# Chunked SSD steps taken in group pairs, with the first projection's matmuls in one run per pair

## The chip, the cores and the metric

One core of a Trainium2 chip runs the whole kernel as one program. The metric is the device time of one execution in microseconds (us); the median of several runs counts. The engines are TensorE (PE in the profile, PEld for its weight loads), VectorE (DVE), ScalarE (ACT), GpSimd (POOL) and SyncE (SP, which issues the loads).

## The reference

One layer of a decoder trunk with two branches, on x of 1024 positions by 1024 channels, all in float32. One branch is a chunked causal gMLP (spatial gating), the other a Mamba-2 SSD mixer with 8 groups of 4 heads (head size 64, state size 128, chunks of 128 positions). Both are projected, gated and merged:

```python
proj = h @ w_in
gm_u, gm_v, gm_z, ssm_z, xbc, dt_raw, g_a, g_b = jnp.split(proj, SPLITS, axis=-1)
y_a = spatial_gating(gelu(gm_u), gelu(gm_v), ...) * silu(gm_z)
xbc = silu(causal_depthwise_conv(xbc, conv_w, conv_b))
xs, bm, cm = jnp.split(xbc, ...)
y_b = ssd_scan(xh, dt, a, bm, cm) + xh * d_skip[:, None]
y_b = rms_norm per group (y_b * silu(ssm_z))
merged = sigmoid(g_a) * (y_a @ w_proj_a) + sigmoid(g_b) * (y_b @ w_proj_b)
return x + gate * (merged @ w_out)        # then a final rms_norm
```

and the scan, per chunk and group:

```python
cb = einsum('bclgn,bcsgn->bcgls', cc, bc)
y_diag = einsum('bcgls,bcgrls,bcsgrp->bclgrp', cb, decay, xd)
chunk_states = einsum('bcsgn,bcgrs,bcsgrp->bcgrpn', bc, decay_to_end, xd)
state = state * chunk_decay + chunk_states                  # from chunk to chunk
y_off = einsum('bclgn,bcgrpn,bcgrl->bclgrp', cc, prev_states, exp(a_cs))
y = y_diag + y_off
```

## The kernel before

**Stages.** First the input projection runs, feature-major, as pairs of column blocks multiplied in a scheme of seven products (p1 to p7). Its products are finished on ScalarE and VectorE and stored in DRAM: `s_d` holds a slab per group and chunk pair (C, B, two blocks of x, two of z), `acs_d` the running sums of the decay, `th_d` the gates, `ya_d` the gMLP's result. Then come the SSD steps, with `y_a @ w_proj_a` (the *first projection*) between them. Then the second projection in seven products (its matmuls are on L1433), the merge, and the output projection. Large products in float32 are taken as three products of a high and a low part.

**The SSD steps.** A step is one group and one pair of chunks (256 positions); there are 32. `order` (L1095) takes two groups side by side: (0,0), (1,0), (0,1), (1,1), and so on, so a group's successive steps are two apart, since the state runs from chunk to chunk. A step has these parts:

- `fetch` (L936): SP loads `dcy` (512 KB, the sums broadcast to all partitions) and `sl`, the slab (768 KB). There are five sets of buffers, so a fetch waits until the step five before is through with its set.
- `decay` (L952): ScalarE makes `ea` (L957), POOL masks dcy (affine select, L960), ScalarE takes the exponentials of dcy in eight pieces (L965).
- `prep` (L967): TensorE multiplies C and B into `pc` and transposes B and x into `pc` and `px`; VectorE scales x into `xd` and `xe` (L981) and multiplies dcy by pc (L985); ScalarE copies B into `bn` (L987).
- `front` (L990): TensorE multiplies `yi` from xd and dcy, and `sp`, the chunks' state sums, from bn and xe; POOL decays the state (L1013) and VectorE adds sp (L1015), for each of the two chunks.
- `back` (L1019): TensorE multiplies `yn` from the states; VectorE makes y1 = yi + D x (L1041) and ym (L1045); POOL adds them and multiplies by z (L1046, L1047), giving `yz`. After a group's odd chunk pairs `post` stores yz as `yb_d` (issued by ScalarE, L88), and squares and sums for the norm follow by the list of later work (`pq`, L1074).

**The first projection** (`proj_a`, L1243) is a generator. A block of 128 output rows takes 24 pieces; a piece is two matmuls `pma` of 128x512, one per half of the positions. At a block's start SP loads `tha` (the gate, two tiles from a ring) and weights; at its end VectorE multiplies tha by pma (L1266) and ScalarE issues the store to `mt_d` (L1268). `draw(n)` takes n pieces.

**What sets the order.** The program is written in the order that L1303 to L1323 says, and a scheduler places it on each engine; parts of a step are marked as urgent. Per step n: its front, four or five pieces (ten for the first three), its back, the preparation of step n + 2, the fetch up to step n + 5, the decays up to n + 3. What remains of the first projection is drawn behind the last step. Each engine works through its own list in order. PSUM has eight banks, handed out in turn by `bank`.

**Places.** The [128, 512] tiles of the stage come from one list of free slots (`room`); `ring(n)` takes n of them and `turn` hands them out in turn: four for tha, three for ea, two each for y1 and ym (L1272). A chunk's state tile is 256 wide and takes, in turn, a slot of its own and places in two other pools (L1273).

Of the kernel before, what the change touches and what calls it, by code (L numbers as in the profile page):

```python
# [8 lines left out]
F32 = mybir.dt.float32  # L9
# [3 lines left out]
ALU = mybir.AluOpType  # L13
# [3 lines left out]
P = 128  # L17
# [18 lines left out]
def hybrid_kernel(  # L36
# [7 lines left out]
    V, A, G, PE = nc.vector, nc.scalar, nc.gpsimd, nc.tensor  # L44
# [25 lines left out]
    def cst(shape, name, dt=F32):  # L70
        return const.tile(shape, dt, name=name, tag=name)
# [3 lines left out]
    def mm(acc, l, r, first=True, last=True):  # L75
        pin(PE.matmul(acc, l, r, start=first, stop=last))  # L76
# [7 lines left out]
    def load(dst, src):  # L84
        pin(nc.sync.dma_start(dst, src))
# [28 lines left out]
    dskt = cst([P, 16], "dskt")  # L114
# [16 lines left out]
    hp = hpool.__enter__()  # L131
# [335 lines left out]
    def bank(name):  # L467

        if pairs_done:
            pairs_done.append(name)  # L470
            if len(pairs_done) % 4 == 2:
                return psum.tile([P, 512], F32, name=name, tag="px", bufs=2)
        return psum.tile([P, 512], F32, name=name, tag="bk", bufs=6)
# [449 lines left out]
    def fac(t, g, s):  # L923

        return t.rearrange("p (c h) -> p c h", h=NH)[:, 2 * s : 2 * s + 2, HPG * g : HPG * (g + 1)]

    NSET = 5
    nstep, nst = [0], [0]

    class Group:  # L930
# [5 lines left out]
        def fetch(self, s):  # L936
            g, nm = self.g, f"{self.g}_{s}"
            n = nstep[0] % NSET
            nstep[0] += 1
            pool, b = (p2r, 2) if n < 2 else (p2q, NSET - 2)  # L940
            dcy = pool.tile([P, HPG, 2, P], F32, name=f"dcy{nm}", tag="dcy", bufs=b)
            load(dcy.rearrange("p h i l -> p (h i l)"),
                 acs_d[g, s].rearrange("h t -> (h t)").unsqueeze(0).to_broadcast([P, HPG * 256]))
            sl = pool.tile([P, 6, 256], F32, name=f"sl{nm}", tag="sl", bufs=b)
            load(sl, s_d[g][:, s])
            if n < 2:
                ea = p2r.tile([P, 2, 256], F32, name=f"ea{nm}", tag="ea", bufs=2)
            else:
                ea = turn(ea_r, f"ea{nm}", F32).rearrange("p (j t) -> p j t", j=2)
            self.pre[s] = (sl, dcy, ea)  # L950
# [39 lines left out]
        def front(self, s):  # L990

            g, nm = self.g, f"{self.g}_{s}"
            sl, dcy, bn, xd, xe, ea = self.pre[s]
            v3 = lambda t: t.rearrange("p (h w) -> p h w", h=HPG)
            yi = bank(f"yi{nm}")
            for i in range(2):
                for h in range(HPG):
                    j, hh = h // 2, h % 2
                    mm(yi[hh * HD : (hh + 1) * HD, j * 256 + i * P : j * 256 + (i + 1) * P],
                       xd[:, i * 256 + h * HD : i * 256 + (h + 1) * HD], dcy[:, h, i, :])  # L1000
            sp = bank(f"sp{nm}")
            self.y[s] = yi
            self.sts = [self.st]
            for i in range(2 if s < NCH // 2 - 1 else 1):
                mm(sp[:, i * 256 : (i + 1) * 256], bn[:, i * P : (i + 1) * P], xe[:, i * 256 : (i + 1) * 256])
            for i in range(2 if s < NCH // 2 - 1 else 1):
                pool, tag, b = st_r[nst[0] % 4 if nst[0] % 4 < 3 else 2]
                nst[0] += 1
                s2 = pool.tile([P, 512 if pool is hp else 256], F32, name=f"st{nm}_{i}", tag=tag, bufs=b)[:, 0:256]
                if self.st is None:  # L1010
                    V.tensor_copy(s2, sp[:, 0:256])
                else:
                    G.tensor_mul(v3(s2), v3(self.st),  # L1013
                                 fac(cd, g, s)[:, i].unsqueeze(2).to_broadcast([P, HPG, HD]))
                    V.tensor_add(s2, s2, sp[:, i * 256 : (i + 1) * 256])  # L1015
                self.st = s2
                self.sts.append(s2)

        def back(self, s):  # L1019

            sl = self.pre[s][0]
            yn = bank(f"yn{self.g}_{s}")
            for i in range(2):
                if self.sts[i] is not None:
                    for j in range(2):
                        mm(yn[:, j * 256 + i * P : j * 256 + (i + 1) * P], self.sts[i][:, j * P : (j + 1) * P],
                           sl[:, 0, i * P : (i + 1) * P])
            self.evacuate(s, self.y.pop(s), yn)
            if s % 2:
                self.post(s // 2)  # L1030

        def evacuate(self, s, yi, yn):

            g, nm = self.g, f"{self.g}_{s}"
            sl, ea = self.pre[s][0], self.pre[s][5]
            if s % 2 == 0:
                self.yz[s // 2] = p2r.tile([P, 2, 512], F32, name=f"yz{nm}", tag="w4", bufs=4)
            yz = self.yz[s // 2][:, :, (s % 2) * 256 : (s % 2 + 1) * 256]
            y1 = turn(y1_r, f"y1{nm}", F32).rearrange("p (j t) -> p j t", j=2)
            for j in range(2):  # L1040
                V.scalar_tensor_tensor(y1[:, j], sl[:, 2 + j], dskt[:, 2 * g + j : 2 * g + j + 1],  # L1041
                                       yi[:, j * 256 : (j + 1) * 256], op0=ALU.mult, op1=ALU.add)
            m = turn(ym_r, f"ym{nm}", F32).rearrange("p (j t) -> p j t", j=2)
            t0 = 0 if s else P
            V.tensor_tensor(m[:, :, t0:], yn.rearrange("p (j l) -> p j l", j=2)[:, :, t0:], ea[:, :, t0:], op=ALU.mult)  # L1045
            G.tensor_add(y1[:, :, t0:], y1[:, :, t0:], m[:, :, t0:])  # L1046
            G.tensor_mul(yz, y1, sl[:, 4:6])  # L1047
# [47 lines left out]
    order = [(2 * r + j, s) for r in range(NG // 2) for s in range(4) for j in range(2)]  # L1095
# [8 lines left out]
    def decays(n):  # L1104
        while done_d[0] < min(n, len(order)):
            g, s = order[done_d[0]]
            groups[g].decay(s)
            done_d[0] += 1
# [18 lines left out]
    room = [f"{nm}{v}{k}" for nm in BN for v in "hl" for k in range(4)]  # L1127

    def take(name, tag=None, dt=F32R):
        return hp.tile([P, 512], dt, name=name, tag=tag or room.pop(0))  # L1130

    def ring(n):

        return [room.pop(0) for _ in range(n)], [0]

    def turn(r, name, dt=F32R):
        tags, at = r
        at[0] += 1
        return take(name, tags[(at[0] - 1) % len(tags)], dt)
# [63 lines left out]
    for n, (name, _, _, d1, d2, g) in enumerate(todo):  # L1203
# [21 lines left out]
        if n + 2 == len(todo):  # L1225
            wspool.__exit__(None, None, None)
            p2xpool = tc.tile_pool(name="p2x", bufs=1, side="right", reuse_waits="tile")
            p2x = p2xpool.__enter__()
# [12 lines left out]
    p2q = p2qpool.__enter__()  # L1241
# [27 lines left out]

    for r in (war_r, wah_r, wal_r):  # L1270
        r[0][0].extend(room.pop(0) for _ in range(2))
    tha_r, ea_r, y1_r, ym_r = (ring(c) for c in (4, 3, 2, 2))  # L1272
    st_r = [(hp, room.pop(0), 1), (p2x, "st", 1), (p2q, "st", 2)]  # L1273
    fetch(4)
    wa_load(1)
    fetch(5)
# [13 lines left out]
    def draw(n):  # L1290
        for _ in range(n):
            left[0] -= next(fill, 1) is None

    def item(f, s):
        with tc.high_priority():
            f(s)
        run_tasks()

    def step(n, *fs):
        for f in fs:  # L1300
            item(getattr(groups[order[n][0]], f), order[n][1])

    draw(6)  # L1303
    for n in range(2):
        step(n, "front")
        draw(10)
    for n in range(len(order)):
        if n > 1:
            step(n, "front")
            draw(10 if n == 2 else 4 + n % 2)  # L1310
        step(n, "back")
        if n + 2 < len(order):
            step(n + 2, "prep")
        fetch(n + 6)
        decays(n + 4)
    while tasks:
        draw(2)
        run_tasks()


    room.extend(ea_r[0] + [st_r[0][1]])
    room.extend(tag for k in range(KT - 2) for tag in ya_tags[k])
    draw(left[0] - 5)  # L1323

# [14 lines left out]
    def slot_tile(name, dt=F32):  # L1339
        tag = room.pop(0)  # L1340
        t = hp.tile([P, 512], dt, name=name, tag=tag)
        tags_of[name] = tag
        return t
# [165 lines left out]
    for u, (nm, k) in enumerate(units):  # L1509
# [22 lines left out]
        if nm in ("p7", "p4") and k % 2 == 0:  # L1532
            n = k // 2 + (4 if nm == "p4" else 0)
# [7 lines left out]
        if k == KT - 1:  # L1541
            for j in range(4):
                with tc.high_priority():
                    if nm == "p1":
                        t = slot_tile(f"c11_{j}")
# [4 lines left out]
                    elif nm in ("p5", "p3"):  # L1550
                        t = slot_tile(f"{nm}_{j}")
# [130 lines left out]
```

## Time and profile before

| | us |
|---|---|
| median of 3 runs | 1427.75 (1426.89 to 1429.42) |
| the profiled execution | 1430.48 |
| its span in the trace | 1428.8 |
| TensorE busy | 1398.2 (98%) |
| VectorE busy | 1025.1 (72%) |
| ScalarE busy | 783.3 (55%) |
| POOL busy, nearly all of it in the SSD stage | 200.0 (14%) |
| mean granted clock of TensorE | 0.997 |

The span runs from the first to the last instruction that the profiler recorded; the execution's own time has 1.7 us more around it. A row of the timeline reads: start in us, length of the group, engine, line, operation, output and inputs with the buffers' numbers left out, sizes, count; in brackets the idle time just before it, and what ended it. A row of the waits reads: engine, what waited, on whom; us in total, how many times, the longest.

### The profile page before, as it was taken

The page shows a single profiled execution, that of the slowest core. Times are in us where ns is not written, and L with a number is a line of the kernel's source. Part 1 is how long each engine was busy: PE and PEld are TensorE (multiplying, and loading weights), DVE is VectorE, ACT ScalarE, POOL GpSimd, SP SyncE. Part 2 cuts the span into 40 slices and gives each one's busy share as a digit, 9 for nine tenths or more (in the row PEclk, how much of TensorE's full clock was granted, in tenths as well). Part 3 has the DMA queues.
Part 4 walks back from the last instruction along what each step waited for, and adds up shares of the span by engine and source line. Part 5 has one row for each costly group of instructions (what it writes and reads, how often), then busy time and mean ns, then how long its engine had stood idle before and what let it go on. Part 6 is the DMA issues. An engine that isn't in the chain of part 4 may idle for free.

```text
span 1428.8 us, 20531 instructions
## 1 busy us (share of the span) xinstructions
PE 1398.2 (98%) x7111; PEld 1157.7 (81%) x7111; DVE 1025.1 (72%) x1812; ACT 783.3 (55%) x1436; POOL 200.0 (14%) x188
## 2 busy tenths in 40 slices
PE   8999999999999999999999999999999999999997
PEld 7788888888888888888888788878888877787886
DVE  4686677777677888788888884488677766948443
ACT  5664576666556655545665555767667533334201
POOL 0000000000000000000000100048878810000000
PEclk9999999999999999999999999999999999999999
DMA  8552333333323687587687764799788567987332
GB/s 268 150 169 82 126 106 108 102 113 103 118 87 107 197 237 220 159 251 225 193 240 214 225 190 148 253 310 314 258 264 305 206 226 266 355 262 280 121 118 74
DMA packets 260460, 276.82 MB, mean 194 GB/s; under 512 B 13596, under 2 KB 210628, under 8 KB 260356
## 3 DMA queue, kind: packets, MB, share of 16 engines
q1 hardware_dynamic: 179364, 195.24, 43.9%
q10 hardware_dynamic: 80992, 80.26, 16.6%
q8 instruction: 56, 0.92, 0.3%
q14 instruction: 48, 0.39, 0.1%
HBM read 191.27 MB, written 84.18 MB: 193 GB/s over the span
## 4 chain that ended last, share of the span: by engine, by line
PE 78%; DMA 9%; DVE 5%; issue 3%; ACT 2%; POOL 2%; SPq 1%; ACTq 0%; POOLq 0%; DVEq 0%
PE xuz L560 6%; PE po L76 6%; PE xcb L560 6%; PE xx L560 5%; PE xz L560 5%; PE x L1433 4%; PE xg L560 4%; PE pma L76 3%; PE yp L1433 3%; PE xv L560 3%; PE yuz L560 3%; PE ycb L560 3%; PE yx L560 3%; PE yz L560 2%; DMA yn<-yb_d 2%
## 5 line engine op out<-in xcount | busy, mean ns | idle before, releaser
L766 POOL TENSOR_TENSOR wog<-wog,gb 128x1024 f32<-128x1024 f32 x8 | 20.3, 2536 | 722.8 <-DVE wbr L800 529.3
L965 ACT ACTIVATE dcy<-dcy,nacs 128x128 f32<-128x128 f32 x256 | 78.4, 390 | 13.4 <-POOL dcy L960 13.3
L960 POOL TENSOR_SCALAR_AFFINE_SELECT dcy<-dcy 128x1024 f32<-128x1024 f32 x32 | 35.0, 1095 | 107.9 <-ACT ea L957 107.7
L957 ACT ACTIVATE ea<-dcy 64x512 f32<-64x512 f32 x64 | 40.1, 627 | 11.4 <-DMA dcy<-acs_d 11.0
L1645 ACT ACTIVATE xr<-r 128x1024 f32<-128x1024 f32 x7 | 7.4, 1061 | 67.2 <-issue 39.7
L878 ACT ACTIVATE ac<-ac 128x1024 f32<-128x1024 f32 x32 | 34.0, 1062 | 17.9 <-DVE ac L876 17.8
L76 PE MATMUL pma<-yh,wah 128*128 128x512 f32 x128 | 43.1, 418 | 0.0
L76 PE MATMUL pma<-yh,wal 128*128 128x512 f32 x128 | 42.6, 414 | 0.0
L1045 DVE TENSOR_TENSOR ym<-yn,ea 128x512 f32<-128x512 f32 (+1 forms) x32 | 19.9, 623 | 30.6 <-PE yn L76 30.6
L1047 POOL TENSOR_TENSOR yz<-y,sl 128x512 f32<-128x512 f32 x32 | 41.5, 1298 | 0.9
L985 DVE TENSOR_TENSOR dcy<-dcy,pc 128x1024 f32<-128x1024 f32 x32 | 39.0, 1217 | 3.3 <-PE pc L79 1.9
L76 PE MATMUL pma<-yl,wah 128*128 128x512 f32 x128 | 40.1, 394 | 0.0
L1046 POOL TENSOR_TENSOR y<-y,ym 128x512 f32<-128x512 f32 (+1 forms) x32 | 36.6, 1143 | 16.7 <-DVE ym L1045 16.6
L76 PEld LDWEIGHTS yn<-sl,st 128*128 128x128 f32 x224 | 30.4, 190 | 9.5 <-POOL yz L1067 3.7
L1644 DVE TENSOR_TENSOR r<-po,xr 128x1024 f32<-128x1024 f32 x7 | 8.6, 1225 | 41.1 <-PE po L76 41.1
L876 DVE SCALAR_TENSOR_TENSOR ac<-c2cb,cwt,ac 128x1023 f32<-128x1023 f32 (+2 forms) x24 | 32.0, 1335 | 7.9 <-ACT ac L874 6.4
L76 PE MATMUL yn<-sl,st 128*128 128x128 f32 x224 | 31.8, 277 | 5.8 <-DVE st L1015 4.6
L1372 DVE SCALAR_TENSOR_TENSOR yn<-yn,par,rb 128x512 f32<-128x512 f32 x32 | 24.0, 749 | 17.2 <-DMA yn<-yb_d 17.1
L876 DVE SCALAR_TENSOR_TENSOR ac<-c2x,cwt,ac 128x1023 f32<-128x1023 f32 (+2 forms) x24 | 30.7, 1280 | 7.6 <-ACT ac L874 6.1
L76 PE MATMUL sp<-xe,bn 128*128 128x256 f32 x112 | 32.6, 408 | 2.8 <-DVE xe L981 1.2
L1635 POOL TENSOR_TENSOR r<-r,fnw 128x256 f32<-128x256 f32 (+1 forms) x3 | 2.8, 918 | 232.4 <-ACT xr L1634 232.4
L76 PE MATMUL yi<-dcy,xd 128*64 128x128 f32 x512 | 35.0, 279 | 0.0
(2810 smaller groups left out, 4406.6 us busy)
## 6 DMA issues: line engine op xcount, KB each, us to landing
sl<-s_d SPq DMA_DIRECT2D x32, 768.0 KB
s_d<-ac ACTq DMA_DIRECT2D x32, 512.0 KB
dcy<-acs_d SPq DMA_DIRECT2D x32, 512.0 KB
aw<-in_ada_w_dram SPq DMA_DIRECT2D x16, 512.0 KB
wbr<-in_w_proj_b_dram SPq DMA_DIRECT2D x64, 128.0 KB
wb_d<-wbb ACTq DMA_DIRECT2D x32, 256.0 KB
wb_d<-wbc ACTq DMA_DIRECT2D x32, 256.0 KB
yb_d<-yz ACTq DMA_DIRECT2D x32, 256.0 KB
```

What stands on the lines that cost most here:

```text
L76: pin(PE.matmul(acc, l, r, start=first, stop=last))
L560: pin(PE.matmul(ps, lw[:, k * P : (k + 1) * P], r[k], start=first and n + k == 0, stop=n == 2 and k == 3, skip_group_check=not first))
L876: V.scalar_tensor_tensor(ac[:, s:], cc[:, : S - s], conv_wt[:, 3 - s, i : i + 1], ac[:, s:], op0=ALU.mult, op1=ALU.add)
L878: A.activation(ac, ac, AF.Silu)
L957: A.activation(ea[hh * HD : (hh + 1) * HD], dcy.rearrange("p (j e) i l -> p e j (i l)", e=2)[hh * HD : (hh + 1) * HD, hh], AF.Exp)
L960: G.affine_select(out=d8, in_=d8, compare_op=ALU.is_ge, fill=-1e30, base=0, pattern=[[0, 2 * HPG], [1, P]], channel_multiplier=-1)
L965: A.activation(dcy[:, h, i, :], dcy[:, h, i, :], AF.Exp, bias=sub[:, i, h : h + 1])
L985: V.tensor_tensor(d3, d3, pc[:, 0:256].unsqueeze(1).to_broadcast([P, HPG, 256]), op=ALU.mult)
L1046: G.tensor_add(y1[:, :, t0:], y1[:, :, t0:], m[:, :, t0:])
L1047: G.tensor_mul(yz, y1, sl[:, 4:6])
L1372: V.scalar_tensor_tensor(t, t, snw[:, n : n + 1], rbs[n // 2, h], op0=ALU.mult, op1=ALU.mult)
L1433: pin(PE.matmul(ps[j], a[:, v, js], r, start=first and n + k == 0, stop=n == 2 and k == KT - 1, skip_group_check=not first))
```

## The change

The unit of the loop becomes a pair of steps: the two groups' steps of the same chunk pair. Per pair the program now has front, front, nine pieces of the first projection in one run (14 for the first pair), back, back, the two preparations of the next pair, the fetches up to step n + 6 (n is the pair's first step), and the decays up to n + 5. Six pieces still lie ahead of the first front. In all 155 pieces are drawn in the loops, where it was 167; the rest goes behind the last step.

Three things go with it. y1 is made at the end of `front` and no longer in `evacuate`. The two states of a step lie in the halves of one [128, 512] tile, out of a ring of four (three slots and one place in another pool). And the ring of tha goes from four slots to two, so that the states' slots come out of the same list.

```diff
             sp = bank(f"sp{nm}")
-            self.y[s] = yi
             self.sts = [self.st]
+            nst[0] += 1
+            both = (p2q.tile([P, 512], F32, name=f"st{nm}", tag="st") if nst[0] % 4 == 0 else
+                    take(f"st{nm}", st_r[nst[0] % 4 - 1], F32))
...
-                pool, tag, b = st_r[nst[0] % 4 if nst[0] % 4 < 3 else 2]
-                nst[0] += 1
-                s2 = pool.tile([P, 512 if pool is hp else 256], F32, name=f"st{nm}_{i}", tag=tag, bufs=b)[:, 0:256]
+                s2 = both[:, i * 256 : (i + 1) * 256]
...
+            self.y[s] = y1 = turn(y1_r, f"y1{nm}", F32).rearrange("p (j t) -> p j t", j=2)
+            for j in range(2):
+                V.scalar_tensor_tensor(y1[:, j], sl[:, 2 + j], dskt[:, 2 * g + j : 2 * g + j + 1],
+                                       yi[:, j * 256 : (j + 1) * 256], op0=ALU.mult, op1=ALU.add)
...
-        def evacuate(self, s, yi, yn):
+        def evacuate(self, s, y1, yn):
...
-            y1 = turn(y1_r, f"y1{nm}", F32).rearrange("p (j t) -> p j t", j=2)
-            for j in range(2):
-                V.scalar_tensor_tensor(y1[:, j], sl[:, 2 + j], dskt[:, 2 * g + j : 2 * g + j + 1],
-                                       yi[:, j * 256 : (j + 1) * 256], op0=ALU.mult, op1=ALU.add)
...
-    tha_r, ea_r, y1_r, ym_r = (ring(c) for c in (4, 3, 2, 2))
-    st_r = [(hp, room.pop(0), 1), (p2x, "st", 1), (p2q, "st", 2)]
+    tha_r, ea_r, y1_r, ym_r = (ring(c) for c in (2, 3, 2, 2))
+    st_r = ring(3)[0]
...
     draw(6)
-    for n in range(2):
-        step(n, "front")
-        draw(10)
-    for n in range(len(order)):
-        if n > 1:
-            step(n, "front")
-            draw(10 if n == 2 else 4 + n % 2)
-        step(n, "back")
+    for n in range(0, len(order), 2):
+        for m in range(2):
+            step(n + m, "front")
+        draw(14 if n == 0 else 9)
+        for m in range(2):
+            step(n + m, "back")
         if n + 2 < len(order):
-            step(n + 2, "prep")
-        fetch(n + 6)
-        decays(n + 4)
+            for m in range(2, 4):
+                step(n + m, "prep")
+        fetch(n + 7)
+        decays(n + 6)
...
-    room.extend(ea_r[0] + [st_r[0][1]])
+    room.extend(ea_r[0] + st_r)
```

In the rows below a name such as yi2_2 is the tile yi of group 2, chunk pair 2; the number behind it is a tile's own. First TensorE, around the preparation of a step of chunk pair 2 of groups 2 and 3. Before: the preparation of (2,2), then the front of the step (3,1), which was prepared a step earlier, then the first projection.

```order
L76 MATMUL pc2_2_9542<-sl2_2_9332 128x128
L79 MATMUL pc2_2_9542<-ident_128,sl2_2_9332 128x128
L79 MATMUL px2_2_9541<-ident_128,sl2_2_9332 128x128 x2
L76 MATMUL yi3_1_9576<-dcy3_1_9240,xd3_1_9476 64x128 x8
L76 MATMUL sp3_1_9585<-xe3_1_9478,bn3_1_9481 128x256 x2
L76 MATMUL pma3_0_9604<-yh00_8360,wah3_0_9272 128x512
```

After, from the end of the second preparation of the pair (2,2), (3,2) on:

```order
L76 MATMUL pc3_2_9580<-sl3_2_9448 128x128
L79 MATMUL pc3_2_9580<-ident_128,sl3_2_9448 128x128
L79 MATMUL px3_2_9579<-ident_128,sl3_2_9448 128x128 x2
L76 MATMUL yi2_2_9632<-dcy2_2_9269,xd2_2_9572 64x128 x8
L76 MATMUL sp2_2_9641<-xe2_2_9574,bn2_2_9577 128x256 x2
L76 MATMUL pq0_1_9652<-ones_133,yz0_2_9071 128x1 x4
L76 MATMUL yi3_2_9662<-dcy3_2_9446,xd3_2_9589 64x128 x8
L76 MATMUL sp3_2_9671<-xe3_2_9591,bn3_2_9594 128x256 x2
L76 MATMUL pq1_1_9682<-ones_133,yz1_2_9081 128x1 x4
L76 MATMUL pma2_0_9368<-yh50_8463,wal2_1_9047 128x512
```

A preparation was followed by another step's front; now both fronts follow directly on the two preparations of their own steps, and the run of pma comes behind them.

VectorE at the same place. Before, two steps follow each other, each with its ym, states, and the preparation's three operations:

```order
L1045 TENSOR_TENSOR ym2_1_9535<-yn2_1_9527,ea2_1_9173 128x512
L1015 TENSOR_TENSOR st2_1_1_9516<-st2_1_1_9516,sp2_1_9510 128x256
L985 TENSOR_TENSOR dcy2_2_9330<-dcy2_2_9330,pc2_2_9542 128x1024
L981 TENSOR_TENSOR xd2_2_9551<-px2_2_9541,dthq_147 128x512
L981 TENSOR_TENSOR xe2_2_9553<-px2_2_9541,dde_148 128x512
L1041 SCALAR_TENSOR_TENSOR y13_1_9623<-sl3_1_9242,dskt_144,yi3_1_9576 128x256 x2
L1015 TENSOR_TENSOR st3_1_0_9588<-st3_1_0_9588,sp3_1_9585 128x256
L1045 TENSOR_TENSOR ym3_1_9626<-yn3_1_9618,ea3_1_9244 128x512
L1015 TENSOR_TENSOR st3_1_1_9591<-st3_1_1_9591,sp3_1_9585 128x256
L985 TENSOR_TENSOR dcy3_2_9410<-dcy3_2_9410,pc3_2_9633 128x1024
```

After, the same place holds both ym, then both preparations, then the states and y1:

```order
L1045 TENSOR_TENSOR ym2_1_9545<-yn2_1_9540,ea2_1_9129 128x512
L1045 TENSOR_TENSOR ym3_1_9556<-yn3_1_9551,ea3_1_9268 128x512
L985 TENSOR_TENSOR dcy2_2_9269<-dcy2_2_9269,pc2_2_9563 128x1024
L981 TENSOR_TENSOR xd2_2_9572<-px2_2_9562,dthq_147 128x512
L981 TENSOR_TENSOR xe2_2_9574<-px2_2_9562,dde_148 128x512
L985 TENSOR_TENSOR dcy3_2_9446<-dcy3_2_9446,pc3_2_9580 128x1024
L981 TENSOR_TENSOR xd3_2_9589<-px3_2_9579,dthq_147 128x512
L981 TENSOR_TENSOR xe3_2_9591<-px3_2_9579,dde_148 128x512
L1015 TENSOR_TENSOR st2_2_9642<-st2_2_9642,sp2_2_9641 128x256
L1075 TENSOR_SCALAR ssq_151<-pq0_1_9652 128x4
L1020 SCALAR_TENSOR_TENSOR y12_2_9649<-sl2_2_9271,dskt_144,yi2_2_9632 128x256 x2
L1020 SCALAR_TENSOR_TENSOR y13_2_9679<-sl3_2_9448,dskt_144,yi3_2_9662 128x256 x2
```

The six operations of two preparations now stand in one run between the pair's ym and its own states; y1 has moved ahead of the ym of its step.

SP's loads around the third block of the first projection, before:

```order
L85 DMA wa4_1_9127<-in_w_proj_a_dram 128x4x128
L85 DMA tha2_0_9129<-th_d_107 128x512
L85 DMA tha2_1_9132<-th_d_107 128x512
L85 DMA dcy2_1_9169<-acs_d_57 128x1024
L85 DMA sl2_1_9171<-s_d2_119 128x1536
L85 DMA dcy3_1_9240<-acs_d_57 128x1024
```

and after:

```order
L85 DMA wa4_1_9364<-in_w_proj_a_dram 128x4x128
L85 DMA tha2_0_9366<-th_d_107 128x512
L85 DMA tha2_1_9369<-th_d_107 128x512
L85 DMA dcy3_2_9446<-acs_d_57 128x1024
L85 DMA sl3_2_9448<-s_d3_120 128x1536
L85 DMA dcy2_3_9451<-acs_d_57 128x1024
```

The kinds of loads stand in the same order; the fetches behind tha2 are now those of a later step, and tha2 takes the slots that the block just before it had.

## Prediction

> **What bounds the kernel now.** I read the engine totals first, then the stage that the change touches, then TensorE's waits in it, then a stretch of its timeline beside VectorE's. The page's head gives the span and each engine's busy time:
>
> ```profile
> span 1428.8 us, 20531 instructions
> PE 1398.2 (98%) x7111; PEld 1157.7 (81%) x7111; DVE 1025.1 (72%) x1812; ACT 783.3 (55%) x1436; POOL 200.0 (14%) x188
> ```
>
> TensorE is busy 98% of the span, so the kernel is TensorE's instruction list plus about 30 us of gaps. The SSD steps lie between 928 and 1150 us. Cut into windows (columns: window, length, busy time of PE, PEld, DVE, ACT, POOL, then the granted clock, the DMA share and GB/s):
>
> ```profile
> 928.00:950.00 22.00, 20.11 (x130) 16.52 (x130) 19.33 (x32) 17.38 (x44) 8.73 (x11) 1.00 1.02 351
> 950.00:1000.00 50.00, 48.19 (x370) 41.89 (x369) 39.54 (x70) 34.07 (x89) 37.09 (x36) 1.00 0.86 295
> 1000.00:1050.00 50.00, 47.04 (x356) 40.73 (x355) 35.69 (x67) 35.10 (x93) 39.16 (x38) 1.00 0.74 249
> 1050.00:1100.00 50.00, 47.31 (x370) 41.63 (x369) 36.54 (x68) 34.24 (x91) 40.41 (x39) 1.00 0.87 296
> 1100.00:1150.00 50.00, 48.27 (x373) 41.97 (x372) 35.78 (x68) 27.41 (x69) 39.32 (x39) 1.00 0.57 197
> ```
>
> TensorE idles 1.89 + 1.81 + 2.96 + 2.69 + 1.73 = 11.1 us of these 222. That is all that a better order of this stage can win, 0.8% of the time. Its waits there:
>
> ```profile
> PE yn L76 <- DVE st L1015: 4.6, 4, 2.2
> PE pc L76 <- issue: 1.9, 1, 1.9
> PE sp L76 <- DVE xe L981: 1.2, 2, 0.6
> PE yn L76 <- POOL yz L1067: 1.2, 1, 1.2
> PE sp L76 <- DVE ssq L1075: 1.0, 1, 1.0
> PE sp L76 <- DVE ym L1045: 0.7, 1, 0.7
> PE pq L76 <- ACT bn L987: 0.6, 1, 0.6
> ```
>
> Eleven waits in 32 steps: most steps have none. The next question is what keeps TensorE fed between a preparation and the front that uses it. Two steps of its timeline:
>
> ```profile
> 956.38 1.05 PE L76 MATMUL yn<-sl,st 128*128 128x128 f32 x8
> 957.26 0.39 PE L76 MATMUL pc<-sl 128*128 128x128 f32 x2
> ...
> 958.46 1.09 PE L76 MATMUL yi<-dcy,xd 128*64 128x128 f32 x16
> 959.48 1.13 PE L76 MATMUL sp<-xe,bn 128*128 128x256 f32 x4
> 960.26 0.81 PE L76 MATMUL pma<-yh,wah 128*128 128x512 f32 x2
> ...
> 968.68 1.05 PE L76 MATMUL yn<-sl,st 128*128 128x128 f32 x8
> 969.57 0.39 PE L76 MATMUL pc<-sl 128*128 128x128 f32 x2
> ```
>
> Two steps take 968.68 - 956.38 = 12.30 us. A preparation lasts 958.46 - 957.26 = 1.20 (its transposes end it), yi 959.48 - 958.46 = 1.02, sp 960.26 - 959.48 = 0.78. The yi behind this preparation is of the step before the prepared one; the prepared step's own yi comes one whole step later. VectorE's rows for the same kind of preparation:
>
> ```profile
> 964.79 1.22 DVE L985 TENSOR_TENSOR dcy<-dcy,pc 128x1024 f32<-128x1024 f32 x1
> 965.92 0.68 DVE L981 TENSOR_TENSOR xd<-px,dthq 128x512 f32<-128x512 f32 x1
> 966.52 0.68 DVE L981 TENSOR_TENSOR xe<-px,dde 128x512 f32<-128x512 f32 x1
> 969.77 0.69 DVE L1045 TENSOR_TENSOR ym<-yn,ea 128x512 f32<-128x512 f32 x1 [1.45 <-PE yn L76]
> 970.71 1.22 DVE L985 TENSOR_TENSOR dcy<-dcy,pc 128x1024 f32<-128x1024 f32 x1 [0.25 <-PE pc L79]
> 974.49 1.28 DVE L1266 SCALAR_TENSOR_TENSOR tha<-tha,pma 128x512 f32<-128x512 f32 x2
> ```
>
> dcy, xd and xe start 1.13 and 0.60 us apart. In the old order that chain (some 3 us) has six for itself and costs TensorE nothing.
>
> **The change part by part.** The matmuls are the same, and so are the instructions of the other engines. What moves is who stands between them.
>
> *yi of the pair's first step.* Let T be the start of the first preparation on TensorE. The second follows at once, so TensorE reaches yi at T + 2 x 1.20 = T + 2.4, or 2.3 without the gap ahead of a yi. VectorE's dcy starts 970.71 - 969.57 = 1.14 behind pc, xd 1.13 later, and lasts 0.68: T + 2.95. From a VectorE end to the matmul that waits for it I add 0.1, as at 948.55 below. So yi starts at T + 3.05 and waits 0.75. This is so in 15 of 16 pairs (the first is prepared earlier): **11.2 us**. Nothing of pma is left to lie there, since all nine pieces stand ahead of the backs.
>
> *yi of the second step.* VectorE's second dcy starts at 1.14 + 1.13 + 0.60 + 0.60 = 3.47, its xd ends at 3.47 + 1.13 + 0.68 = 5.28, and yi can start at 5.38. TensorE is there at 3.05 + 1.02 + 0.78 = 4.85, or at 4.46 in the last chunk pair of a group, where sp is half as long. In the fronts of chunk pairs 0 and 2 the sums of squares stand in between, and a row of them covers it:
>
> ```profile
> 989.89 0.95 PE L76 MATMUL pq<-ones,yz 128*128 128x1 f32 x8
> ```
>
> The other eight wait 4 x 0.5 and 4 x 0.9: **5.6 us**.
>
> *Banks.* A pair now holds seven of the eight PSUM banks or more (px, pc, yi and sp of one step while the other's are prepared, two pma), where a step shared them with its neighbour alone. The nearest rows, the two waits of sp for xe above (0.6 each), are of this kind. Between nothing and 0.6 for each of 15 pairs (0 to 9) I take **2.5**, near the few that the rows show.
>
> *Start of the stage.* The wait of 1.9 us in the list above is this one, with VectorE's row before it:
>
> ```profile
> 947.77 0.68 DVE L981 TENSOR_TENSOR xe<-px,dde 128x512 f32<-128x512 f32 x1
> 948.55 0.46 PE L76 MATMUL pc<-sl 128*128 128x128 f32 x2 [1.89 <-issue]
> ```
>
> The preparation for the second pair waits for the first pair's xe (end 948.45). Before, 6 + 10 + 10 pieces lay ahead of the first back; now it is 6 + 14, so six pieces (12 matmuls of 0.23, 2.8 us) fewer cover it. Half of that is filled by the second front and the second back: 1.9 + 1.4 = **3.3** (bounds 1.9 and 4.7).
>
> *Old waits.* Of the other 9.2 us, those of yn for st came of a draw too short for the chain sp, st. Two fronts and nine pieces now lie there, so I keep a quarter, **2.3** (bounds 0 and 9.2).
>
> *SP's queue.* The ring of tha goes from four slots to two. Its next load now waits until the last block's product (DVE L1266 above) has been stored, and every dcy and sl fetch issued later stands behind it. ScalarE's issue of that store, the landing of a store and of a dcy in the chain of waits, and the three operations on a dcy that has landed:
>
> ```profile
> 975.69 0.33 ACTq L1268 DMA_DIRECT2D mt_d<-tha  x1
> 992.98 6.82 DMA yb_d<-yz
> 1007.85 7.38 DMA dcy<-acs_d
> 964.78 1.25 ACT L957 ACTIVATE ea<-dcy 64x512 f32<-64x512 f32 x2
> 969.80 1.09 POOL L960 TENSOR_SCALAR_AFFINE_SELECT dcy<-dcy 128x1024 f32<-128x1024 f32 x1 [1.03 <-ACT ea L957]
> 962.42 2.45 ACT L965 ACTIVATE dcy<-dcy,nacs 128x128 f32<-128x128 f32 x8 [1.77 <-POOL dcy L960]
> ```
>
> From a block's last matmul: product 1.4, issue 1, landing 6.8, so 9.2 until SP is free; then 1 for the two loads, dcy 7.4, ea 1.25, select 1.1, exps 2.45: 22.4 us until that dcy may be multiplied. It belongs to the second step of the next pair, whose turn comes at 12.3 + 3.5 + the pair's own waits of 0.8 = 16.6 behind this pair's T. A block ends 3.5 to 5.8 us ahead of T (pieces left in the draw x 0.46, plus two yn of 1.05), so it is from 0 to 2.3 us late, at five places (the loads of blocks two to six). Half of 2.3 is 1.2 each: **6** (bounds 0, if those stores land in half the time, and 20, if the selects on POOL and the exps on ScalarE that stand behind it in order hold up the states as well).
>
> *At nothing.* The states that share a tile: the same copies, multiplications and additions, and yn still waits for the half that it reads; the cover is the nine pieces (4.2 us), and without it a yn would pay up to the 2.2 of the list. y1 made in the front: the same two VectorE instructions, behind the second xe; VectorE is busy 79% of a window at most from 950 on, and what waits for y1 is POOL's sum behind the backs, nine pieces later.
>
> *The tail.* The loops draw 155 pieces instead of 167; 12 (5.6 us) go behind the last step. The stage behind it waits like this:
>
> ```profile
> 1166.35 0.50 PE L1433 MATMUL x<-p1bh,p1a 128*128 128x512 f32 x1 [1.43 <-DVE tha L1266]
> 1216.91 0.76 PE L1433 MATMUL yp<-p5bh,p5a 128*128 128x512 f32 x1 [2.31 <-issue]
> 1200.00:1250.00 50.00, 47.69 (x199) 37.93 (x198) 46.95 (x75) 16.48 (x28) 0.00 (x0) 0.97 0.99 368
> ```
>
> The first waits for the last product, which stays last, and in 1200 to 1250 VectorE (94%) and the DMA (0.99) are as full as TensorE. More matmuls ahead give VectorE a little lead: **-0.4** (bounds 0 and -3.7, both waits).
>
> *Sum.* 11.2 + 5.6 + 2.5 + 3.3 + 2.3 + 6 = 30.9 us of gaps where 11.1 were, less 0.4: +19.4. The profiled execution took 1430.48 (span 1428.8 and 1.7 around it), 2.7 above the median of 1427.75; gaps carry over from one execution to another, so I add to the median: **1447**.
>
> **The rivals.**
> 1. *Faster.* All of the old 11.1 goes, the tail's 3.7 too, and only the first yi's 11.2 come: 1427.75 - 14.8 + 11.2 = 1424. For it: two fronts and nine pieces cover a state chain better than one and four or five. Against it: eight second fronts whose xd is late by VectorE's own rows. It decides at 14.8 / 15 = 1.0 us of new waits a pair, and VectorE's chain alone gives 0.75. Chance 0.09.
> 2. *The loop through SP, POOL and ScalarE.* A late dcy holds the selects and exps behind it, those hold states and bn, and the next fetches come later again: the 20 for the 6, so 1461. For it: POOL is busy 74 to 81% in these windows and has little to catch up with. Against it: each fetch has a pair's lead. Chance 0.20.
> 3. *The waits are covered*, because VectorE reaches the preparations earlier than its rows say or the scheduler's order leaves other matmuls there: new and old gaps equal, 1428. Against it: the order on TensorE is pc, px, yi without a matmul between. Chance 0.08.
> 4. *The clock.* In the window 1200 to 1250 a wait of 2.31 goes with a granted clock of 0.97, so 0.03 x 50 = 1.5 us; the stage's own windows keep 1.00 with a wait of 2.2 in them. If each of 15 pairs set off such a dip: 22 on top, 1469. Chance 0.03.
>
> The Trainium skill, page "TensorE: Matmul & The Clock Gate", section "HAM oscillation — how this bites in real kernels", wants no idle gap of TensorE above about 3.4 us, because the clock falls behind one; by that rule gaps of 0.75 leave the clock alone, and the rows of 950 to 1150 agree (1.00 with gaps to 2.2). Its section "A second HAM failure mode: psum-queue depth-cycling" speaks against this change: short idles between groups of matmuls, set off by cycling through PSUM banks, made the clock swing there; that is rival 4, and no run here shows it in this stage.
>
> **How the numbers follow.** The forecast has the remaining 0.60; with its terms between their bounds it lies at 1432 to 1459. The range adds rival 2 and leaves out 1, 3 and 4 (0.20): 1431 to 1463. A measurement of this kernel can tell about 0.2% (2.9 us) from no change. Faster by more: rival 1 and a little of 3, 0.10. Within: the rest of 3 and a little of the forecast, 0.09. Slower: 0.81.
>
> **What would show it.** Right: about 15 waits of yi for VectorE's xd (or the bank's xe) near 0.75, eight more at the second yi; yn's waits for st nearly gone; TensorE idle some 31 us in the stage; SP waiting for a store ahead of the tha loads; 12 more pieces behind the last step. Wrong: yi starting right behind px, TensorE idle under 15 us in the stage, or waits of yn and pc larger than those of yi, which would put the cost in fetches and states instead of the missing cover.

## The result, and the profile after

| | before | after |
|---|---|---|
| median, us (4 runs each) | 1428.59 | 1474.57 |
| ratio, 95% interval | | 1.0306 (1.029 to 1.0322) |
| profiled execution, its span, us | 1430.48, 1428.8 | 1474.75, 1473.0 |
| TensorE busy, us | 1398.2 | 1413.6 |
| mean granted clock | 0.997 | 0.986 |

The change costs 46 us, not the 19 that were forecast, and lies above the range. All times and ratios in this document leave out one slow execution (2014.72 us at a granted clock of 0.654, of the run with the squares placed later). The page's head of after:

```profile
span 1473.0 us, 20574 instructions
PE 1413.6 (96%) x7111; PEld 1166.2 (79%) x7111; DVE 1028.1 (70%) x1812; ACT 785.4 (53%) x1436; POOL 197.8 (13%) x188
```

The span grew by 44.2 us. TensorE idles 1473.0 - 1413.6 = 59.4 us of it, where it was 30.6: 28.8 more. The other 15.4 is *busy* time, for the same 7111 matmuls. So a third of the loss is no wait at all: the same instructions took longer. The windows of after (columns as in the prediction's table of windows) say where and why:

```profile
928.00:950.00 22.00, 18.60 (x141) 15.16 (x139) 20.50 (x34) 17.52 (x45) 11.08 (x12) 1.00 0.91 322
950.00:1000.00 50.00, 42.56 (x305) 36.10 (x302) 33.34 (x59) 30.50 (x81) 30.63 (x31) 0.93 0.63 225
1000.00:1050.00 50.00, 43.60 (x312) 37.05 (x312) 31.15 (x56) 26.61 (x68) 32.88 (x33) 0.97 0.70 248
1050.00:1100.00 50.00, 43.75 (x318) 37.79 (x318) 30.66 (x58) 31.71 (x84) 33.94 (x34) 0.93 0.76 265
1100.00:1150.00 50.00, 41.35 (x308) 35.15 (x306) 32.41 (x58) 29.65 (x76) 30.42 (x31) 0.97 0.61 214
1150.00:1200.00 50.00, 46.48 (x273) 39.24 (x272) 22.31 (x42) 12.37 (x30) 25.45 (x24) 0.90 0.39 131
```

The granted clock, 1.00 in every window of this stage before, is still 1.00 in the first and 0.90 to 0.97 in the others. Over the whole span 0.014 of 1473.0 is 20.6 us, and 0.003 of 1428.8 was 4.3: 16.3 us more, close to the extra busy time of 15.4.

The windows of before and after do not hold the same work, since the steps now end later: the last yi runs at 1174 and not at 1146. So here is the whole stage, from 928 to the first product of the second projection (at 1163.42 before, at 1201.34 after), and what follows it, beside the forecast's sum:

| us | before | after | more | forecast |
|---|---|---|---|---|
| the stage, TensorE idle | 11.1 | 37.0 | 25.9 | 19.8 |
| the stage, TensorE busy (1657 matmuls at a granted clock of 1.00, then 1647 at 0.94) | 224.3 | 236.3 | 12.0 | 0 |
| from there to the end of the span | 265.4 | 271.7 | 6.3 | -0.4 |

The waits of TensorE from 928 to 1200:

```profile
PE px L79 <- DVE ym L1045: 7.7, 3, 2.7
PE yi L76 <- DVE xd L981: 7.4, 5, 3.7
PE sp L76 <- ACT bn L987: 6.6, 6, 3.1
PE yi L76 <- issue: 5.4, 5, 2.0
PE yi L76 <- DVE xe L981: 2.7, 2, 1.4
PE yi L76 <- POOL st L1013: 2.0, 2, 1.4
PE yi L76 <- POOL y L1046: 1.9, 3, 0.7
PE yi L76 <- POOL yz L1047: 1.4, 1, 1.4
PE pc L76 <- DVE st L1015: 0.3, 1, 0.3
```

Two things stand in this list. yi waits 18 times, 20.8 us in all, where it never waited before. And px, which should be ready to go, waits three times, over 2.3 us each, for VectorE's ym. The releasers beside yi differ (DVE, POOL, issue), but the place is one: behind the pair's own preparations. (At 1007.45, for one, yi is put down to POOL's y, but VectorE's xd had ended 0.10 before it started.)

The wait of px is worth following back, because it begins on another queue. These rows are of after's timeline, one engine behind the other (the stores that ScalarE issues, SP, ScalarE, POOL, VectorE, TensorE):

```profile
1003.54 0.81 ACTq L1268 DMA_DIRECT2D mt_d<-tha  x2
...
996.51 3.27 SPq L85 DMA_DIRECT2D wa<-in_w_proj_a_dram  x2
1008.15 0.95 SPq L85 DMA_DIRECT2D tha<-th_d  x2
1009.21 0.37 SPq L85 DMA_DIRECT2D dcy<-acs_d  x1
...
1015.71 1.27 ACT L957 ACTIVATE ea<-dcy 64x512 f32<-64x512 f32 x2 [6.23 <-DMA dcy<-acs_d]
1020.54 0.60 ACT L1169 CAST wah<-wa 128x512 fp32r<-128x512 f32 x1
...
1017.05 1.09 POOL L960 TENSOR_SCALAR_AFFINE_SELECT dcy<-dcy 128x1024 f32<-128x1024 f32 x1 [4.97 <-ACT ea L957]
...
1018.76 0.42 DVE L1015 TENSOR_TENSOR st<-st,sp 128x256 f32<-128x256 f32 x1 [5.93 <-POOL st L1013]
1021.17 0.69 DVE L1170 TENSOR_TENSOR wal<-wa,wah 128x512 fp32r<-128x512 f32 x1 [1.99 <-ACT wah L1169]
1021.78 1.28 DVE L1045 TENSOR_TENSOR ym<-yn,ea 128x512 f32<-128x512 f32 x2
...
1022.52 0.44 PE L79 MATMUL px<-ident,sl 128*128 128x128 f32 x2 [2.68 <-DVE ym L1045]
1024.84 1.98 PE L76 MATMUL yi<-dcy,xd 128*64 128x128 f32 x16 [1.34 <-DVE xd L981]
```

SP is through with the weights at 999.8 and stands still until 1008.15: the load of tha waits for the store issued at 1003.54. The dcy behind it is issued at 1009.21 and reaches ScalarE at 1015.7, where ea has waited 6.23. ScalarE works in order, so the cast of the weights behind ea (wah) is late; POOL's select waits 4.97 and the states stand behind it; VectorE's wal waits for the cast, and both ym stand behind wal. The px of the second preparation needs a bank that ym still reads. TensorE waits 2.68, then 1.34 for xd; and the yi that then runs takes 1.98, where the same 16 matmuls took 1.09 before.

The end of the stage shows the same queue once more:

```profile
1168.12 24.40 SPq L85 DMA_DIRECT2D tha<-th_d  x4
1192.62 0.38 SPq L85 DMA_DIRECT2D rb<-rs_d  x1
...
1209.55 0.79 PE L1432 MATMUL x<-p1bh,p1a 128*128 128x512 f32 x1 [5.05 <-DVE tha L1266]
```

The last block's tha holds the first loads of the second projection (rb, yn, p1r) until 1192.62; TensorE gets there at some 1200 and waits 1.54 and 5.05 in its first products, where it waited 1.43 in all. The 5.05 end with the first projection's last product, which VectorE reaches only at 1208.22, behind its work on these late loads.

### The profile page after: what moved, and what is told of

It reads as the page before. It is cut to its first block, busy times and chain, and to the rows that moved or that the text cites. A ratio compares the mean times of both kernels' runs of the same rounds, so it can differ in the third digit from the quotient of the medians.

```text
span 1473.0 us, 20574 instructions
## 1 busy us (share of the span) xinstructions
PE 1413.6 (96%) x7111; PEld 1166.2 (79%) x7111; DVE 1028.1 (70%) x1812; ACT 785.4 (53%) x1436; POOL 197.8 (13%) x188
## 5 line engine op out<-in xcount | busy, mean ns | idle before, releaser
L76 PE MATMUL yi<-dcy,xd 128*64 128x128 f32 x512 | 41.4, 311 | 20.8 <-DVE xd L981 7.4
L957 ACT ACTIVATE ea<-dcy 64x512 f32<-64x512 f32 x64 | 40.1, 626 | 33.4 <-DMA dcy<-acs_d 32.7
L76 PEld LDWEIGHTS yi<-dcy,xd 128*64 128x64 f32 x512 | 33.0, 156 | 29.2 <-issue 8.9
L76 PE MATMUL sp<-xe,bn 128*128 128x256 f32 x112 | 37.8, 460 | 6.6 <-ACT bn L987 6.6
L76 PE MATMUL pma<-yh,wah 128*128 128x512 f32 x128 | 40.0, 393 | 0.0
L1371 DVE SCALAR_TENSOR_TENSOR yn<-yn,par,rb 128x512 f32<-128x512 f32 x32 | 23.9, 747 | 21.2 <-DMA yn<-yb_d 21.2
L1015 DVE TENSOR_TENSOR st<-st,sp 128x256 f32<-128x256 f32 x48 | 19.6, 416 | 26.3 <-POOL st L1013 16.1
```

What stands on the lines that cost most here:

```text
L957: A.activation(ea[hh * HD : (hh + 1) * HD], dcy.rearrange("p (j e) i l -> p e j (i l)", e=2)[hh * HD : (hh + 1) * HD, hh], AF.Exp)
L1371: V.scalar_tensor_tensor(t, t, snw[:, n : n + 1], rbs[n // 2, h], op0=ALU.mult, op1=ALU.mult)
```

## The experiments

Ratios are to the kernel before on the same chip, with 95% intervals. In brackets behind a difference of ratios stands the same in us (times 1428.6).

**tha loaded later.** Each block but the first and last loads its tha when 12 of its 24 pieces are done.

```diff
             for h in range(2):
-                th = turn(tha_r, f"tha{dd}_{h}", F32)
-                load(th, th_d[dd * P : (dd + 1) * P, h * 512 : (h + 1) * 512])
-                ths.append(th)
                 pms.append(bank(f"pma{dd}_{h}"))
             for k in range(KT):
+                if k == (4 if 0 < dd < KT - 1 else 0):
+                    for h in range(2):
+                        th = turn(tha_r, f"tha{dd}_{h}", F32)
+                        load(th, th_d[dd * P : (dd + 1) * P, h * 512 : (h + 1) * 512])
+                        ths.append(th)
```

> The changed kernel, but the loads of tha for blocks two to seven are issued when the block is half done (12 of 24 pieces later), when the store that they wait for has long landed; the ring stays at two. Theory A (SP's queue: the tha load waits for the store of the block before, dcy comes late behind it, ScalarE's ea waits for that dcy, and states, bn and the weights' casts stand behind ea): the waits of px for ym (7.7 us), most of sp for bn (6.6), the yi wait of 3.7 and at least four of the five clock dips go: 20 to 28 us faster than the changed kernel, about 1450. Theory B (missing cover: yi directly behind its own preparation): 1470 to 1475. Theory C (ScalarE's squares, which wait for the store of yb_d): 1470 to 1475.

Measured: 1466.81 us, 1.0238 (1.0197 to 1.0279). All waits of px for ym are gone, as theory A said, and the longest yi wait falls from 3.7 to 2.0. But the gain is a third to a half of the expected 20 to 28: 0.0068 (9.7 us). The clock did not come back: the four runs show 0.986, 0.993, 0.987 and 0.986, where after shows 0.982 to 0.986. sp still waits for bn (7.7 us in 6 waits). At the end SP still holds the second projection's first loads, until 1187.99, though TensorE waits only 0.64 and 1.17 in its first products.

**Four pieces behind the preparations.**

```diff
-        draw(14 if n == 0 else 9)
+        draw(10 if n == 0 else 5)
...
+            draw(4)
```

> The changed kernel, but four of the nine pieces stand behind the two preparations, ahead of the fronts (five stay ahead of the backs). Theory B: the waits of yi for xd and xe (some 0.7 to 1.4 each, 16 us in all without the one of 3.7) go, and with them the dips that follow: 1450 to 1458. Theory A: the late dcy still holds everything and the waits only move: 1463 to 1472.

Measured: 1458.18 us, 1.0192 (1.0164 to 1.0221), at the upper end of what theory B said: 0.0114 (16.3 us) back. The waits of yi fall from 20.8 us to about 5. What theory A is about stays and shows elsewhere: a preparation waits for its slab,

```profile
PE pc L76 <- DMA sl<-s_d: 7.4, 2, 6.1
PE sp L76 <- ACT bn L987: 7.4, 4, 3.7
PE x L1433 <- DVE tha L1266: 5.8, 1, 5.8
```

So both theories hold a part.

**Squares placed later.** `later(5, self.squares, ...)` becomes `later(10, ...)`.

> The changed kernel, but the squares of yz are placed ten ticks of the list of later work behind the store of yb_d, not five, so that ScalarE reaches them when the store has landed. Theory C: ScalarE's 20.7 us of waiting for those stores go, and ea, the casts and bn behind them come earlier: 1460 to 1466. Theories A and B: 1471 to 1477.

Measured: 1481.33 us (the median of three runs), 1.0365 (1.0327 to 1.0402): slower than the changed kernel. ScalarE's waits for the yb_d stores fall only from 20.7 to 17.6 us, and its waits for dcy rise from 32.7 to 36.2. Theory C falls. Its granted clock was 0.977 to 0.981 against 0.982 to 0.986 in after, by the means some 8 us and so about the whole difference; what lowered it was not followed.

**The three things beside the order, in the old loop.**

> The old loop (one step after the other) with the three things that go with the change: y1 in the front, the shared state tile, and the ring of two for tha. Theory A: the ring holds SP's queue in the old order as well, so a part of the loss is there: 1433 to 1445. Theory B: all of the loss is in the order of the pairs: 1427 to 1431.

Measured: 1445.23 us, 1.0101 (1.0071 to 1.0132), at the upper end of what theory A said. A part of the loss has nothing to do with pairs.

**The ring alone, in the kernel before.**

```diff
-    tha_r, ea_r, y1_r, ym_r = (ring(c) for c in (4, 3, 2, 2))
+    tha_r, ea_r, y1_r, ym_r = (ring(c) for c in (2, 3, 2, 2))
```

> The kernel before with one number changed: two slots for tha, not four. Theory A (the ring is what costs in the things that go with the change): 1.007 to 1.012 of before, as the run with all three of them (1.010). Rival (y1 in the front or the shared state tile costs): within 1.003 of before.

Measured: 1442.80 us, 1.0081 (1.0056 to 1.0106). One number of the change costs 11.6 us in a kernel that is otherwise untouched. The run with all three things lies within its interval, so y1 in the front and the shared tile cost nothing that can be told (with these two intervals, less than some 0.4% would not show). New in its list of waits is the same kind of victim as in after, a px whose bank is held:

```profile
PE px L79 <- ACT bn L987: 3.0, 1, 3.0
PE sp L76 <- DVE ym L1045: 2.3, 1, 2.3
```

**The later loads in the old loop.**

> The old loop with y1 in the front, the shared state tile and the ring of two, but tha of blocks two to seven loaded when the block is half done. Theory A: what is left is the end, where the last block's tha still holds the second projection's first loads (a wait of 5.9 us and its dip): 1.003 to 1.006 of before. Rival: 1.008 to 1.012, as without the later loads.

Measured: 1443.57 us, 1.0092 (1.0072 to 1.0112): a miss for theory A. In the old order the later loads return nothing that can be told; the profile still has the end's wait (4.5 us of x for tha) and five waits of yn for st (6.1 us). How the ring's cost divides in the old loop stays open.

**Both causes taken away.** Four pieces behind the preparations, tha loaded later, and the last block's tha in two slots that the states have left:

```diff
-                        th = turn(tha_r, f"tha{dd}_{h}", F32)
+                        th = (take(f"tha{dd}_{h}", room.pop(3), F32) if dd == KT - 1 else
+                              turn(tha_r, f"tha{dd}_{h}", F32))
```

> The order of the pairs with four of nine pieces behind the preparations, tha loaded when a block is half done, and the last block's tha in two slots that the states have left. If missing cover, the hold of SP's queue and the end are the three causes and add up (16, 8 and some 6): 1441 to 1448, ratio 1.006 to 1.014. If bn on ScalarE stands late whatever the rest does, its waits (7 us and their dips) stay: 1449 to 1456.

Measured: 1434.27 us, 1.0017 (1.0002 to 1.0032). 0.0289 of the 0.0306 is gone (41.3 us): more than the sum of the parts that I had expected. The waits of TensorE up to 1210:

```profile
PE sp L76 <- ACT bn L987: 7.0, 7, 1.9
PE yi L76 <- DVE xe L981: 2.8, 3, 2.0
PE x L1436 <- DVE tha L1269: 2.3, 1, 2.3
PE yi L76 <- issue: 2.0, 1, 2.0
PE yp L1436 <- DVE tri L1089: 1.6, 1, 1.6
PE yi L76 <- POOL y L1046: 1.5, 2, 1.3
```

What remains in the stage is mostly sp waiting for bn, which stands in ScalarE's queue behind exponentials, ea and the squares; none of it is over 2.

**Back, preparation, back, preparation.** The same, with each back followed by a preparation.

> As the run before it, and each back is followed by its own preparation (back, prep, back, prep), so that VectorE starts the first dcy a back (1 us) earlier: 2 to 5 us faster than that run if yi's or sp's waits are still set by VectorE's chain; no difference if they are set by ScalarE's queue.

Measured: 1434.79 us, 1.0021 (1.0008 to 1.0034): no difference. In its profile the waits for bn are 2.3 us, and the end's wait is 3.7. The two profiled executions lie 6.8 us apart (1439.22 and 1432.46) where the medians are equal, so whether one wait takes the place of the other can't be told from them.

**The ring's cost taken away, the cover left missing.** The changed kernel with tha loaded later and the last block's tha in the states' slots.

> The order of the pairs as changed (nine pieces ahead of the backs, none behind the preparations), with tha loaded late and the last block's tha in two of the states' slots: the ring's cost taken away, the missing cover left. If the two causes add, it lies as far below the changed kernel as the run with both lies below the run with cover alone (1.0192 - 1.0017 = 0.0175): 1.013 of before, some 1449. If each hides the other, it stays near the run with the late loads alone: 1.020 to 1.024, 1460 to 1466.

Measured: 1454.70 us, 1.0161 (1.0144 to 1.0177). It lies between the two expectations, nearer to adding. With this the four corners are there: neither cause taken away 1.0306, cover given alone 1.0192, the ring's cost taken away alone 1.0161, both 1.0017. The ring is worth 0.0145 (20.7 us) without cover and 0.0175 with it, the cover 0.0114 and 0.0144 (20.6 us). They add: the 0.0030 more is within the noise of four ratios. These prices hold what the clock loses to each cause, not the waits alone.

**Ten idle transposes.** The run above, with work in the place of the first yi's wait that serves nothing:

```diff
+            if g % 2:
+                for _ in range(5):
+                    for i in range(2):
+                        tp(px[:, i * 256 + P : i * 256 + 256], sl[:, 3, i * P : (i + 1) * P], ident)
```

> The same, with ten more transposes (of x into px, the same values again, some 0.1 us each) behind every second preparation: they do nothing but keep TensorE busy while it would wait for VectorE's first xd. If the short waits cost more than their length because the clock falls behind them, the dips go and it is 6 to 12 us faster than the run without them, though it has 160 instructions more. If the clock falls for another reason, or the waits cost only their length, it is the same or up to 3 us slower.

Measured: 1457.90 us, 1.0188 (1.0169 to 1.0207): 3 to 4 us slower than without them. The waits of yi, 21.2 us in the run above (seven rows of its list), are down to 8.6:

```profile
PE yi L76 <- issue: 3.0, 2, 1.5
PE yi L76 <- DVE xd L985: 1.8, 3, 1.4
PE yi L76 <- POOL yz L1051: 1.8, 2, 1.4
PE yi L76 <- POOL yz L1071: 1.3, 2, 0.7
...
PE yi L76 <- DVE xe L985: 0.7, 3, 0.3
```

and the clock hardly moves: 0.994 to 0.996 in the four runs against 0.992 to 0.993. So the frequent short waits of yi, taken by themselves, cost about their length and not a dip each. The dips (short stretches at half the clock) that this run still has come behind single waits of sp for bn (2.43, 1.39) and of x for tha (3.12).

**More cover.** As in the run with back, preparation, back, preparation, but five pieces behind the preparations in seven of the pairs.

> Back, preparation, back, preparation, five pieces ahead and four behind as before, five behind in the first seven pairs (162 pieces in the loops): the most cover that the pairs can have with the late loads. If the stage still waits for cover: 2 to 5 us below the run with 4 (1434.8), so 1.000 of before or less. If the rest (bn, the second projection's start, which waits for the last tha in VectorE's order) sets the time: 1.001 to 1.003, no better than the kernel before.

Measured: 1435.70 us, 1.0032 (1.0019 to 1.0045). More cover brings nothing; no version with pairs beats the kernel before.

**The end alone.** The changed kernel with the last block's tha in the states' slots, nothing else.

> The changed kernel with one thing undone: the last block's tha takes two slots that the states have left, so that SP can issue the second projection's first loads without waiting for the store of the block before. From the two runs with late loads (1.0238 without this, 1.0161 with it) the end alone is worth 0.0077: if it adds to the rest, 1.021 to 1.025 of before, some 1459 to 1466. If the hold during the steps sets the end anyway (the last steps are late, and with them the last stores), 1.028 to 1.031.

Measured: 1470.97 us, 1.0270 (1.0241 to 1.0298): between the two expectations, a miss. Alone it returns 0.0036 (5 us), 3.7 of them in the stretch behind the stage (268.0 where after has 271.7); SP's first load for the second projection comes at 1181.98 and not at 1192.62. With the later loads it comes at 1165.50, and the two together return 0.0145. The hold during the steps and the hold at the end are one queue, and the first delays the second. Not all of the 0.0145 is explained by that: see the tail below.

## Why the prediction was wrong, step by step

The span grew by 44.2 us where the sum had 19.4. Of the 24.8 that are missing, 12.0 are matmuls that took longer in the stage, which the sum put at nothing; 6.7 lie behind the stage, which it put at -0.4; 6.1 are gaps in the stage. So the step that failed most is the clock: only gaps were added up, and the clock stood as a rival for itself.

- **The direction and the missing cover were right.** "yi of the pair's first step" waits in 15 of 16 pairs, as said: 18.1 us where 11.2 stood, with the one of 3.71 that the late dcy makes. "yi of the second step" was wrong: 5.6 stood for eight waits, and of the 2.8 in the trace 1.99 is one wait in the first pair; sp behind it waits for bn instead (6.6 us), which I had not priced. ScalarE copies bn in its own order, behind exponentials, ea and squares. Together the two stood at 16.8 and the trace has 20.8; taking the cover's absence away returns 16.3 to 20.6 us, with what the clock gives back in it.
- **The old waits** were right in kind: yn's waits for st are gone altogether (I kept 2.3).
- **Banks and the start of the stage.** Banks stood at 2.5. px waits 7.7 for one, but these three waits come of the late dcy: none is left with the later loads. The start stood at 3.3 for a wait of pc. None is in the list; the yi of 1.99 stands in its place.
- **SP's queue: the latency was right, the overlap was not.** It stood at 6 with bounds 0 and 20. The chain above takes 20.8 us from the block's product (999.80) to the end of the exponentials (1020.63), where 22.4 stood. But the working followed one dcy to its own multiplication and asked how late that was (0 to 2.3). ScalarE reaches that dcy's ea *before* its turn and waits there, and everything behind it waits as well, although it has nothing to do with that dcy. That was rival 2, with a chance of 0.20. The later loads take 8.3 us of gaps out of the stage (37.0 to 28.7) and return 9.7; with the end it is 20.7.
- **The tail was wrong.** It was put at -0.4, because the last product "stays last", and it came out at 6.3. SP's queue was followed only inside the stage. The ring of two also holds the last tha's load, and behind it stand the first loads of the second projection. Undoing this alone returns 5 us. With the later loads in place it moves the ratio from 1.0238 to 1.0161 (11.0 us), but in the profiles only 3.0 of these lie behind the stage (271.1 and 268.1). Most of the rest is the clock in the steps (0.95 in the stage, then 0.98), ahead of what that edit touches; why it rose there is not shown.
- **The clock was left out.** Rival 4 had it at 0.03, set off by yi's short waits. It fell, by 16.3 us over the span. In after all six dips up to 1262 come with a long wait: three of px, one each of sp, yi and x, of 2.37 to 5.05 us. In two of them a short wait of yi close behind adds 0.95 and 0.65 (the last section shows how waits add up). That SP's queue alone did it is not shown: with the later loads px's waits are gone and the clock is still 0.986 or 0.987 in three runs of four, with dips behind shorter waits (1.98 of yi; 1.34 of yi with 1.78 of sp). It is at 0.991 or more in all runs where the later loads and the end's slots come together.
- **At nothing** was right: state tile and y1 are within what the runs can tell.
- **The range** failed because rivals 2 and 4 were taken as alternatives to the sum and to each other. They came together, and 1461 and 1469 were each too low. The upper end was also added up wrong: the terms at their upper bounds are 11.2 + 5.6 + 9 + 4.7 + 9.2 + 20 = 59.7 us of gaps, which gives 1476 and not 1459 (1462 with 6 for SP's queue).

What stays open: why bn's waits stay at 7 us through most variants, why the clock fell further with the later squares, what raised it where both holds of SP's queue were undone, and how the ring's 11.6 us divide in the old loop.

## What to carry to other kernels

When a change gives a buffer ring fewer slots, follow the load that will now wait along its whole queue, into the next stage too, and then along every in-order engine that waits for what is queued behind it. Ask of each operation not when its result is needed but when its engine reaches it, since all that stands behind it stops there. And a matmul engine's waits are to be priced at more than their length where they are long or lie close together: look at the granted clock behind them.

## What the runs showed of the hardware that was not expected

A wait of TensorE of about 2 us or more is mostly followed by matmuls at half the clock for some microseconds. In the fourteen profiles, from 928 to 1262, I set each wait of 1.2 us or more beside the granted clock of the 5 us behind it and counted a dip where that is below 0.95:

| wait, us | waits | with a dip |
|---|---|---|
| 1.2 to 1.6 | 61 | 9 |
| 1.6 to 2.0 | 28 | 11 |
| 2.0 to 2.9 | 26 | 20 |
| 2.9 to 6.1 | 19 | 19 |

Some of the short ones follow a longer wait closely and share its dip. Two rows from the same kind of place, the first from the old loop with the later loads, where a wait of 2.82 left the clock at 1.00, the second from after, where 3.06 halved it (sp's four matmuls took 1.13 at full clock):

```profile
1036.71 0.68 PE L76 MATMUL yn<-sl,st 128*128 128x128 f32 x4 [2.82 <-DVE st L1015]
```

```profile
1072.85 2.08 PE L76 MATMUL sp<-xe,bn 128*128 128x256 f32 x4 [3.06 <-ACT bn L987]
```

The Trainium skill, page "TensorE: Matmul & The Clock Gate", section "HAM oscillation — how this bites in real kernels", gives about 3.4 us as the gap to stay under. All 13 waits above 3.4 here agree with it, but the six from 2.9 to 3.4 and most between 2.0 and 2.9 lowered the clock too, so in this kernel the limit that the measurement supports is nearer to 2 us.

What looks like chance between 1.6 and 2.9 is in part a matter of where a wait falls. In each of the fourteen profiles the stretches at half the clock begin on a grid of slices of 3.41 us and last one to four slices. I added up TensorE's idle time slice by slice, from 928 to 1262: of the 54 slices at full clock with 1.8 us or more of it, 51 were followed by half the clock; of the 1210 others, 8. So what counts here is the idle time inside one slice, not the length of one wait. The wait of 3.06 puts 2.45 into one slice; the wait of 2.82 is cut by an edge into 0.9 and 1.9, and is one of the three exceptions.
